# Cross-attention: softmax weights of two heads turned together in row halves, the last head's scores between the V products

## The chip, the cores and the metric

The kernel runs on one core of one Trainium2 chip. The metric is device time in microseconds of one execution; the kernel before takes 1437.06 us (median of three runs, 1436.53 to 1437.17). Five engines work side by side on the core: PE (matrix products; its weight loads are listed apart as PEld), ACT (pointwise functions and casts), DVE (vector arithmetic), POOL (a second, slower vector engine) and SP (which here only starts transfers). Every engine runs its own list of instructions in order and waits on the others by semaphores.

## The reference, cut to what matters

A trunk of two layers on 512 positions of width 1024 in float32. Layer 0 begins with a gated DeltaNet, layer 1 with a convolution module; each layer then has a cross-attention into a fixed memory of 256 rows and a squared-ReLU MLP. The change touches the two cross-attentions alone:

```python
def memory_cross_attention(h, mem_h, w_q, w_kv, w_o):
    B, S, _ = h.shape
    M = mem_h.shape[1]
    q = (h @ w_q).reshape(B, S, XA_HEADS, XA_HEAD_DIM)
    kv = (mem_h @ w_kv).reshape(B, M, 2, XA_HEADS, XA_HEAD_DIM)
    k, v = kv[:, :, 0], kv[:, :, 1]
    s = jnp.einsum("bshd,bmhd->bhsm", q, k).astype(jnp.float32) * (XA_HEAD_DIM ** -0.5)
    p = jax.nn.softmax(s, axis=-1).astype(v.dtype)
    o = jnp.einsum("bhsm,bmhd->bshd", p, v).reshape(B, S, D_MODEL)
    return o @ w_o
```

There are 4 heads of width 256. For one head, the scores are 512 x 256 (positions by memory rows).

## The kernel before, in words

Activations lie with the channels on the 128 partitions and the 512 positions along the row. Each float32 operand of a product is split into a high part (a rounded copy, made by ACT) and a low part (the rest, made by DVE), and each product is done as three: high by high, high by low, low by high. So a 128-row step of a product is three PE rows, and each weight tile of 128 x 1024 needs a cast on ACT (`wh`, L259) and a subtraction on DVE (`wl`, L73).

In a cross-attention, `q_mm(m)` makes 128 of the 1024 query channels (24 PE rows of 512 columns); `q_ev(m)` scales them out of PSUM and splits them. A head takes two such tiles. `sc(h)` makes the scores of head h: four blocks of 128 positions, two to a PSUM bank, 24 PE rows of 256 columns. For each bank DVE takes the negative row maximum (L1128), ACT the exponential and the row sum (L1133, two instructions), DVE the reciprocal (L1136), and POOL multiplies (the `pexp` tile). The scores have the positions on the partitions, but the V product needs the memory rows there, so `tr(h)` turns the weights of a head on PE: eight turns of 128 x 128 against the identity (L1147), four into each of two PSUM banks, one bank for each half of the memory rows; `split` then makes the high part (`pTh`, ACT) and the low part (`pTl`, DVE), each in one instruction of 512 columns. `pv(h)` is the V product, 12 PE rows for each head, whose two outputs are split again (`aoh` on ACT, `aol` on DVE). The output projection `proj(w, outs, ps, k0, k1)` takes those as its steps k: steps 0 and 1 are of head 0, 2 and 3 of head 1, and so on. The first two output tiles (`w0`, `w1`) are begun before all heads are there; six more follow.

The lines at the end of `xattn` write the order of this work out by hand, and PE follows it as written. The order on ACT, DVE and POOL is made by a scheduling layer that takes what is ready in the order of the program and puts it into the engine's list; two engines that read the same PSUM bank are put one behind the other by it. PSUM has 8 banks, shared by all of these tiles (tag `ps`).

Another helper exists before the change: `turn_in` turns a 128 x 128 block in two instructions, one for each half of 64 partitions, each into a PSUM bank of its own (L309). It serves in the DeltaNet, in the convolution module and in the MLP; the tiles turned by it there are `vt`, `ogT`, `lnT` and `hT`. `turned_of` and `by_half` name the pieces in which such a pair of banks is read back.

Of the kernel before, what the change touches and what calls it, by code (L numbers as in the profile page):

```python
# [8 lines left out]
F32 = mybir.dt.float32  # L9
F32R = mybir.dt.float32r  # L10
AF = mybir.ActivationFunctionType
ALU = mybir.AluOpType
AX = mybir.AxisListType

P = 128
# [23 lines left out]
def tile_trunk(ctx, tc, xT, memT, x_d, mem_d, prm_d, adt_d, bdw_d, tap_d, fin_d, first_d, w_ab, w_kq, w_v, w_z, w_dno, w_pw1, w_pw2,  # L39
               w_q, w_k, w_vv, w_o, w_up, w_dn, yT):  # L40
    nc = tc.nc
    pe, act, dve, pool = nc.tensor, nc.scalar, nc.vector, nc.gpsimd
# [11 lines left out]
    def nm(s):  # L54
        cnt[0] += 1
        return f"{s}_{cnt[0]}"

    def slot(dt=F32, s="u", shape=(P, NT)):
        return up.tile(list(shape), dt, tag="u", name=nm(s))

    def psum(s="ps"):
        return psp.tile([P, NT], F32, tag="ps", name=nm(s))

    def small(n, s="sm"):
        return sp.tile([P, n], F32, tag="sm", name=nm(s))

    def const(shape, s, dt=F32):
        return cp.tile(list(shape), dt, tag=s, name=s)
# [3 lines left out]
    def tt(e, o, a, b, op):  # L72
        r = e.tensor_tensor(out=o, in0=a, in1=b, op=op)  # L73
        if e is pool:
            last_pool[:] = [r]
        return r

    def stt(o, a, s, b, op0, op1):
        return dve.scalar_tensor_tensor(out=o, in0=a, scalar=s, in1=b, op0=op0, op1=op1)  # L79
# [6 lines left out]
    def c4(t):  # L86
        return t.rearrange("p (c i) -> p c i", c=4)

    def over_i(t4, n=P):
        return t4.unsqueeze(2).to_broadcast([P, t4.shape[1], n])  # L90
# [34 lines left out]
    ident = const([P, P], "ident")  # L125
# [148 lines left out]
    def wnext(key, hf):  # L274
        i = ws["next"]
        assert order[i] == (key, hf), (order[i], key, hf)
        while ws["load"] <= need[min(i + NRAW + 1 + 2 * (order[i][0][0] in ("up", "dn7")), len(order) - 1)]:
            wload()
        ready = NW - (order[i] == (("do", 1), 1) or i in (conv0 - 1, conv0)) if i > 2 else (1, 2, 1)[i]
        while ws["split"] < min(i + ready, len(order)):  # L280
            wsplit()
        ws["next"] += 1
        return ws["hl"].pop(i)
# [3 lines left out]
    def behind_merge():  # L287
        return tc.issue_after(ahead[0].ins) if ahead else nullcontext()
# [17 lines left out]
    def turn_in(pss, at, src):  # L306
        for half in range(2):
            r = slice(64 * half, 64 * half + 64)
            pe.transpose(pss[half][:, at:at + 64], src[r, :], ident[r, r])  # L309

    def turned_of(pss, k):
        return [c4(ps[:, 256 * k:256 * k + 256]) for ps in pss]

    def by_half(t):
        return [c4(t)[:, :, 64 * half:64 * half + 64] for half in range(2)]

    def mm3(ps, wk, xk, first, last):
        (wh, wl), (xh, xl) = wk, xk
        pe.matmul(ps, wh, xh, start=first, stop=False)  # L319
        pe.matmul(ps, wh, xl, start=False, stop=False)  # L320
        pe.matmul(ps, wl, xh, start=False, stop=last)  # L321

    def wk(w, k):
        c = slice(k * P, (k + 1) * P)
        return w[0][:, c], w[1][:, c]

    def proj(w, xs, ps, k0=0, k1=KT, inside=None):
        for k in range(k0, k1):
            mm3(ps, wk(w, k), xs[k], k == 0, k == KT - 1)
            if inside and k in inside:  # L330
                inside[k]()
# [45 lines left out]
    def split(src, s):  # L377
        h = slot(F32R, s + "h")
        with behind_merge():
            act.copy(h, src)  # L380
        lo = slot(F32R, s + "l")
        tt(dve, lo, src, h.bitcast(F32), ALU.subtract)
        return h, lo
# [708 lines left out]
    def phased(t):  # L1092
        return t.rearrange("p (t s) -> p s t", s=PH)

    def by_phase(t):
        return t.rearrange("p (s t) -> p s t", s=PH)

    def xattn(layer, norm, hres, nxt):
        K, V = KV[layer]
        xs = norm.xs  # L1100
        st = {}

        def q_mm(m, inside=None):
            st["ps", m] = psum("q")
            proj(wnext(("xq", layer, m // 2), m % 2), xs, st["ps", m], inside=inside)

        def q_ev(m):
            qf = slot(s="qf")
            stt(qf, st.pop(("ps", m)), 1.0 / 16, norm.rb, ALU.mult, ALU.mult)
            st["q", m] = split(qf, "q")  # L1110

        def sc(h):
            pr = []
            kh, kl = K[h]
            for tp in range(2):
                ps = psum("sc")
                mxn = small(2)
                for i in range(2):
                    t = tp * 2 + i
                    t_ = slice(t * P, (t + 1) * P)  # L1120
                    o = ps[:, i * 256:(i + 1) * 256]
                    for d in range(2):
                        ks = slice(d * 256, (d + 1) * 256)
                        qh, ql = st["q", 2 * h + d]
                        pe.matmul(o, qh[:, t_], kh[:, ks], start=d == 0, stop=False)
                        pe.matmul(o, qh[:, t_], kl[:, ks], start=False, stop=False)
                        pe.matmul(o, ql[:, t_], kh[:, ks], start=False, stop=d == 1)
                dve.tensor_reduce(out=mxn, in_=ps.rearrange("p (t m) -> p t m", t=2), op=ALU.max,  # L1128
                                  axis=AX.X, negate=True)
                pe_ = slot(s="pexp")  # L1130
                sm = small(2)
                for i in range(2):
                    act.activation(pe_[:, i * 256:(i + 1) * 256], ps[:, i * 256:(i + 1) * 256], AF.Exp,  # L1133
                                   bias=mxn[:, i:i + 1], accum_out=sm[:, i:i + 1])
                rs = small(2)
                dve.reciprocal(rs, sm)  # L1136
                p3 = pe_.rearrange("p (t m) -> p t m", t=2)
                tt(pool, p3, p3, over_i(rs, 256), ALU.mult)
                pr.append(pe_)
            st["p", h] = pr  # L1140

        def tr(h):
            pts = []
            for mt in range(2):
                ps = psum("pT")
                for t in range(4):
                    pe.transpose(ps[:, t * P:(t + 1) * P],  # L1147
                                 st["p", h][t // 2][:, (t % 2) * 256 + mt * P:(t % 2) * 256 + (mt + 1) * P],
                                 ident)
                pts.append(split(ps, "pT"))  # L1150
            st["pt", h] = pts

        outs = [None] * 8

        def pv(h):
            for d in range(2):
                ps = psum("pv")
                for mt in range(2):
                    vh, vl = V[mt, h // 2]
                    vs = slice((h % 2) * 256 + d * P, (h % 2) * 256 + (d + 1) * P)  # L1160
                    mm3(ps, (vh[:, vs], vl[:, vs]), st["pt", h][mt], mt == 0, mt == 1)
                outs[2 * h + d] = split(ps, "ao")

        new = []

        def o_ev(m, ps):
            hn = slot(s="h")
            if layer == 0:
                tt(dve, by_phase(hn), phased(ps), phased(hres[m]), ALU.add)
            else:  # L1170
                tt(dve, hn, ps, hres[m], ALU.add)
            new.append(hn)
            nxt.add(m, hn)

        def ow(m):
            return wnext(("xo", layer, m // 2), m % 2), psum("xo")

        q_mm(0)
        q_mm(1, {1: norm.stat})
        q_ev(0)  # L1180
        q_ev(1)
        q_mm(2); q_ev(2); sc(0)
        q_mm(3); q_ev(3)
        q_mm(4); tr(0); q_ev(4); sc(1)
        q_mm(5); q_ev(5); pv(0)
        q_mm(6); tr(1); q_ev(6); sc(2)
        q_mm(7); q_ev(7); pv(1)
        tr(2)
        w0, p0 = ow(0)
        proj(w0, outs, p0, 0, 4)  # L1190
        sc(3)
        pv(2)
        w1, p1 = ow(1)
        proj(w1, outs, p1, 0, 6)
        tr(3)
        proj(w0, outs, p0, 4, 6)
        pv(3)
        for k in (6, 7):
            proj(w0, outs, p0, k, k + 1)
            proj(w1, outs, p1, k, k + 1)  # L1200
        o_ev(0, p0)
        o_ev(1, p1)
        for m in range(2, 8):
            w, ps = ow(m)
            proj(w, outs, ps)
            o_ev(m, ps)
        return new
# [645 lines left out]
    for gq in range(2):  # L1853
# [9 lines left out]
        for i in range(4):  # L1863
            h = 4 * gq + i
# [55 lines left out]
    h = []  # L1920
# [11 lines left out]
    h = xattn(0, n1, h, n2)  # L1932
    n3 = Norm("cv_norm")
    h, rest = mlp7(0, n2, h, n3, lambda: (mem_gain(1, 0), taps(NTAP, *range(9)), selections()))
    n4 = Norm("xa_norm1")
    h = conformer(n3, h, n4, rest)
    n5 = Norm("mlp_norm1")
    h = xattn(1, n4, h, n5)


# [163 lines left out]
```

## Time and profile before

| | us |
|---|---|
| median of three runs | 1437.06 |
| the profiled execution: its own time | 1436.97 |
| the profiled execution: span from first to last instruction | 1435.3 |
| PE busy | 1426.3 (99%) |
| DVE busy | 1047.7 (73%) |
| ACT busy | 763.0 (53%) |
| POOL busy | 244.2 (17%) |
| cross-attention of layer 0, first q product to the last of the first two output tiles | 346.2 to about 428 |
| the same in layer 1 | about 985 to 1067 |

The granted clock of PE is 0.999 of full speed. In the timeline a PE row of 512 columns is listed with 0.39 us, yet the next one starts 0.23 us later: rows overlap, and what counts is the distance from start to start. The chain of waits (the work that ended last, followed back) lists each step by that distance. "PE xo L320 0.32" there is a row that held up the next by 0.32 us. In names such as `pT<-ident,pexp`, the tile left of the arrow is written and those right of it are read.

### The profile page before, as it was taken

Reading aid. Unit: us, or ns where it says so; the run is one execution under the profiler, and the core shown is the slowest. Engines: PE = TensorE matmul, PEld = TensorE weight load, DVE = VectorE, ACT = ScalarE, POOL = GpSimd, SP = SyncE. Lnnn points to the kernel's source line nnn. Section 1 sums busy time; section 2 is a strip of 40 time slices with the busy share of each in tenths; the row PEclk is TensorE's granted clock in tenths of the full one; section 3 lists DMA queues with packets and bytes.
Section 4 is the critical chain, followed back from the end, with each engine's and each line's share of the span. In section 5 each row is a group of like instructions: output and inputs, shape, how many; then the busy total and the mean of one; then the engine's idle time right before and its main releaser. Section 6 shows DMA issues by size and latency. Waiting matters only on the chain.

```text
span 1435.3 us, 20462 instructions
## 1 busy us (share of the span) xinstructions
PE 1426.3 (99%) x7786; PEld 1191.7 (83%) x7786; DVE 1047.7 (73%) x1625; ACT 763.0 (53%) x1282; POOL 244.2 (17%) x248
## 2 busy tenths in 40 slices
PE   9999999999999999999999999999999999999998
PEld 7887888888888888888888888888888888888886
DVE  5989989867555765767679799976555766767677
ACT  6657855655444454435345656464444644444354
POOL 1212200102113000000000298111112010010101
PEclk9999999999999999999999999999999999999999
DMA  8232235523214567575866448642215476675853
GB/s 292 82 118 66 70 102 162 173 93 103 74 33 129 149 179 179 141 202 134 205 158 219 154 137 291 221 149 89 74 57 134 123 184 166 150 205 138 222 147 88
DMA packets 71860, 207.83 MB, mean 145 GB/s; under 512 B 15441, under 2 KB 16593, under 8 KB 71761
## 3 DMA queue, kind: packets, MB, share of 16 engines
q1 hardware_dynamic: 60960, 169.22, 36.0%
q0 software_dynamic: 9792, 35.66, 14.4%
q10 hardware_dynamic: 1008, 1.64, 0.3%
q8 instruction: 61, 1.00, 0.3%
q14 instruction: 39, 0.31, 0.1%
HBM read 203.28 MB, written 3.21 MB: 144 GB/s over the span
## 4 chain that ended last, share of the span: by engine, by line
PE 90%; DVE 6%; DMA 1%; ACT 1%; issue 1%; POOL 0%; SPq 0%; ACTq 0%; DVEq 0%
PE up L319 8%; PE up L320 8%; PE up L321 8%; PE dn L1263 7%; PE dn L1264 7%; PE dn L1265 7%; PE pw L319 3%; PE pw L320 3%; PE pw L321 3%; PE xo L320 2%; PE q L319 2%; PE xo L319 2%; PE q L320 2%; PE q L321 2%; PE xo L321 2%; PE h L319 1%
## 5 line engine op out<-in xcount | busy, mean ns | idle before, releaser
L259 ACT CAST wh<-raw 128x1024 fp32r<-128x1024 f32 x259 | 271.5, 1051 | 338.0 <-issue 106.6
L73 DVE TENSOR_TENSOR wl<-raw,wh 128x1024 fp32r<-128x1024 f32 (+1 forms) x250 | 306.6, 1229 | 92.7 <-ACT wh L259 91.2
L319 PE MATMUL up<-xh,wh 128*128 128x512 f32 x512 | 199.3, 389 | 0.0
L321 PE MATMUL up<-xh,wl 128*128 128x512 f32 x512 | 199.2, 389 | 0.0
L320 PE MATMUL up<-xl,wh 128*128 128x512 f32 x512 | 199.2, 389 | 0.0
L319 PEld LDWEIGHTS up<-xh,wh 128*128 128x128 f32 x512 | 96.1, 188 | 20.1
L321 PEld LDWEIGHTS up<-xh,wl 128*128 128x128 f32 x512 | 96.1, 188 | 20.0
L320 PEld LDWEIGHTS up<-xl,wh 128*128 128x128 f32 x512 | 96.1, 188 | 19.8
L244 POOL DMA_DIRECT2D t<-w_dn x48 | 42.2, 916 | 375.6 <-DVE wl L73 278.4
L1263 PE MATMUL dn<-wh,ah 128*128 128x512 f32 (+1 forms) x260 | 100.6, 387 | 0.0
L1265 PE MATMUL dn<-wl,ah 128*128 128x512 f32 (+1 forms) x260 | 100.5, 386 | 0.0
L1264 PE MATMUL dn<-wh,al 128*128 128x512 f32 (+1 forms) x260 | 100.4, 386 | 0.0
L79 DVE SCALAR_TENSOR_TENSOR rl<-up,rb 128x512 f32<-128x512 f32 x64 | 44.1, 690 | 58.6 <-PE up L321 58.6
L259 ACT CAST wh<-t 128x1024 fp32r<-128x1024 f32 x44 | 46.5, 1056 | 57.6 <-PE dn L1264 43.7
L73 DVE TENSOR_TENSOR wl<-t,wh 128x1024 fp32r<-128x1024 f32 x44 | 53.7, 1223 | 30.7 <-ACT wh L259 27.2
L73 POOL TENSOR_TENSOR sq<-sq,sq 128x512 f32<-128x512 f32 x26 | 42.8, 1646 | 167.8 <-ACT sq L447 150.6
L73 DVE TENSOR_TENSOR acc<-acc,dn 128x512 f32<-128x512 f32 x99 | 66.6, 681 | 1.0
L319 PE MATMUL h<-xh,wh 128*128 128x512 f32 x160 | 63.8, 399 | 0.0
L1546 DVE SCALAR_TENSOR_TENSOR ca<-xn,prm,ca 128x512 f32<-128x512 f32 x82 | 60.8, 751 | 3.9 <-ACT ca L1543 2.3
L321 PE MATMUL h<-xh,wl 128*128 128x512 f32 x160 | 62.4, 390 | 0.0
L320 PE MATMUL h<-xl,wh 128*128 128x512 f32 x160 | 62.3, 389 | 0.0
L73 DVE TENSOR_TENSOR al<-u,ah 128x512 fp32r<-128x512 f32 x64 | 44.1, 689 | 21.3 <-ACT ah L380 21.3
(425 smaller groups left out, 3493.1 us busy)
## 6 DMA issues: line engine op xcount, KB each, us to landing
raw<-w_dn SPq DMA_DIRECT2D x68, 512.0 KB, 4.6
raw<-w_up SPq DMA_DIRECT2D x64, 512.0 KB, 4.9
t<-w_dn POOLq DMA_DIRECT2D x48, 512.0 KB, 6.4
tap<-tap SPq DMA_DIRECT2D x48, 256.0 KB, 5.7
raw<-w_pw SPq DMA_DIRECT2D x24, 512.0 KB, 4.1
raw<-w_dn POOLq DMA_DIRECT2D x20, 512.0 KB, 7.1
raw<-w_k SPq DMA_DIRECT2D x16, 512.0 KB, 3.9
raw<-w_vv SPq DMA_DIRECT2D x16, 512.0 KB, 5.7
```

What stands on the lines that cost most here:

```text
L73: r = e.tensor_tensor(out=o, in0=a, in1=b, op=op)
L79: return dve.scalar_tensor_tensor(out=o, in0=a, scalar=s, in1=b, op0=op0, op1=op1)
L244: nc.gpsimd.dma_start(out=t, in_=a, accum_op=ALU.add)
L259: ins = [act.copy(h, raw)]
L319: pe.matmul(ps, wh, xh, start=first, stop=False)
L320: pe.matmul(ps, wh, xl, start=False, stop=False)
L321: pe.matmul(ps, wl, xh, start=False, stop=last)
L1263: pe.matmul(ps, xh, w[0][:, s], start=opens and k == 0, stop=False, skip_group_check=True)
L1264: pe.matmul(ps, xl, w[0][:, s], start=False, stop=False, skip_group_check=True)
L1265: pe.matmul(ps, xh, w[1][:, s], start=False, stop=k == 3, skip_group_check=True)
L1546: first["tap"] = dve.scalar_tensor_tensor(out=a, in0=src, scalar=w, in1=a, op0=ALU.mult, op1=ALU.add)
```

## The change

`tr` now takes two heads. It asks for four PSUM banks, turns both heads with `turn_in` (32 turns of 64 partitions by 128 columns, in place of 16 turns of 128 x 128), and then reads the banks back in pieces of 256 columns: for each head and half of the memory rows two copies on ACT and two subtractions on DVE, in place of one and one. In one bank lie both halves of the memory rows for one half of the positions. The order of the steps is another: q tiles 4 to 7 follow each other with only the scores of head 1 between; heads 0 and 1 are turned behind them; then the scores of head 2, V of head 0, the scores of head 3, V of head 1, four steps of the first output tile, the turn of heads 2 and 3, four steps of the second output tile, V of heads 2 and 3, and the steps that are left. What is computed is the same.

```diff
-        def tr(h):
-            pts = []
-            for mt in range(2):
-                ps = psum("pT")
-                for t in range(4):
-                    pe.transpose(ps[:, t * P:(t + 1) * P],
-                                 st["p", h][t // 2][:, (t % 2) * 256 + mt * P:(t % 2) * 256 + (mt + 1) * P],
-                                 ident)
-                pts.append(split(ps, "pT"))
-            st["pt", h] = pts
+        def tr(hs):
+            pss = [[psum("pT") for _ in range(2)] for _ in hs]
+            for h, ps in zip(hs, pss):
+                for mt in range(2):
+                    for t in range(4):
+                        turn_in(ps, (4 * mt + t) * 64,
+                                st["p", h][t // 2][:, (t % 2) * 256 + mt * P:(t % 2) * 256 + (mt + 1) * P])
+            for h, ps in zip(hs, pss):
+                st["pt", h] = []
+                for mt in range(2):
+                    ph, pl = slot(F32R, "pTh"), slot(F32R, "pTl")
+                    for o, lo, x in zip(by_half(ph), by_half(pl), turned_of(ps, mt)):
+                        act.copy(o, x)
+                        tt(dve, lo, x, o.bitcast(F32), ALU.subtract)
+                    st["pt", h].append((ph, pl))
...
-        q_mm(4); tr(0); q_ev(4); sc(1)
-        q_mm(5); q_ev(5); pv(0)
-        q_mm(6); tr(1); q_ev(6); sc(2)
-        q_mm(7); q_ev(7); pv(1)
-        tr(2)
+        q_mm(4); q_ev(4); sc(1)
+        q_mm(5); q_ev(5)
+        q_mm(6); q_ev(6)
+        q_mm(7); q_ev(7)
+        tr((0, 1))
+        sc(2)
+        pv(0)
+        sc(3)
+        pv(1)
         w0, p0 = ow(0)
         proj(w0, outs, p0, 0, 4)
-        sc(3)
+        tr((2, 3))
+        w1, p1 = ow(1)
+        proj(w1, outs, p1, 0, 4)
         pv(2)
-        w1, p1 = ow(1)
-        proj(w1, outs, p1, 0, 6)
-        tr(3)
+        pv(3)
         proj(w0, outs, p0, 4, 6)
-        pv(3)
+        proj(w1, outs, p1, 4, 6)
         for k in (6, 7):
```

**How it moves the rows.** On PE, in layer 0, behind q tile 4, the rows before were these (`pT` the turned weights, `pexp` the weights, `sc` the scores):

```order
L1147 MATMUL pT_4142<-ident,pexp_4045 128x128 x2
L1147 MATMUL pT_4142<-ident,pexp_4067 128x128 x2
L1147 MATMUL pT_4151<-ident,pexp_4045 128x128 x2
L1147 MATMUL pT_4151<-ident,pexp_4067 128x128 x2
L1125 MATMUL sc_4166<-Kh_2732,qh_4026 128x256
```

and now, behind q tile 7, they begin so:

```order
L319 MATMUL q_4266<-xh_3901,wh_4195 128x512
L320 MATMUL q_4266<-xl_3903,wh_4195 128x512
L321 MATMUL q_4266<-xh_3901,wl_4196 128x512
L309 MATMUL pT_4303<-ident,pexp_4045 128x64
L309 MATMUL pT_4304<-ident,pexp_4045 128x64
```

Eight turns of one head behind q tile 4 became 32 turns of two heads behind q tile 7, half as wide, the two partition halves in turn into two banks.

On DVE, in layer 0, behind the eviction of q tile 7, the rows before were these (`aol`: the low part of V of head 1, `pTl`: of the turned weights of head 2, `sm`: maxima and reciprocals of head 3):

```order
L79 SCALAR_TENSOR_TENSOR qf_4399<-q_4368,rb_3961 128x512
L73 TENSOR_TENSOR wl_4448<-raw_4270,wh_4447 128x1024
L73 TENSOR_TENSOR ql_4403<-qf_4399,qh_4401 128x512
L73 TENSOR_TENSOR aol_4414<-pv_4405,aoh_4412 128x512
L73 TENSOR_TENSOR aol_4425<-pv_4416,aoh_4423 128x512
L73 TENSOR_TENSOR pTl_4434<-pT_4427,pTh_4432 128x512
L73 TENSOR_TENSOR pTl_4443<-pT_4436,pTh_4441 128x512
L1128 TENSOR_REDUCE sm_4465<-sc_4464 128x2
L1136 RECIPROCAL sm_4483<-sm_4480 128x2
```

and now they are these (`pTl` of heads 0 and 1, then the maxima of head 2):

```order
L73 TENSOR_TENSOR ql_4301<-qf_4297,qh_4299 128x512
L73 TENSOR_TENSOR pTl_4340<-pT_4303,pTh_4339 128x4x64
L73 TENSOR_TENSOR pTl_4340<-pT_4304,pTh_4339 128x4x64
L73 TENSOR_TENSOR pTl_4346<-pT_4303,pTh_4345 128x4x64
L73 TENSOR_TENSOR pTl_4352<-pT_4305,pTh_4351 128x4x64
L73 TENSOR_TENSOR pTl_4346<-pT_4304,pTh_4345 128x4x64
L73 TENSOR_TENSOR pTl_4352<-pT_4306,pTh_4351 128x4x64
L73 TENSOR_TENSOR pTl_4358<-pT_4305,pTh_4357 128x4x64
L1128 TENSOR_REDUCE sm_4364<-sc_4363 128x2
L73 TENSOR_TENSOR pTl_4358<-pT_4306,pTh_4357 128x4x64
L1136 RECIPROCAL sm_4382<-sm_4379 128x2
L1128 TENSOR_REDUCE sm_4386<-sc_4385 128x2
```

Two wide subtractions of one head became eight half as wide of two heads, and the first maximum of head 2 stands behind seven of them. Behind these rows stand the second reciprocal of head 2, the first maximum of head 3, both `aol` of head 0, the rest of head 3's softmax, and both `aol` of head 1. ACT's list has the same pattern: eight `pTh` copies, the exponentials of head 2, two `aoh`, the exponentials of head 3, two `aoh`. POOL's rows and their order are the same as before, and so are SP's.

## The prediction

> **What bounds the kernel now.** I read the page's busy times and its chain first, then what PE waited for, then PE's time in the stretches that the change touches.
>
> ```profile
> PE 1426.3 (99%) x7786; PEld 1191.7 (83%) x7786; DVE 1047.7 (73%) x1625; ACT 763.0 (53%) x1282; POOL 244.2 (17%) x248
> PE 90%; DVE 6%; DMA 1%; ACT 1%; issue 1%; POOL 0%; SPq 0%; ACTq 0%; DVEq 0%
> PE warm L131 <- POOL ones L128: 1.2, 1, 1.2
> PE mg L780 <- ACT w L790: 0.5, 1, 0.5
> PE rb L421 <- DVE rstd L469: 0.3, 1, 0.3
> 376.80:394.20 17.40, 17.40 (x93) 14.97 (x92) 9.04 (x14) 7.38 (x16) 2.08 (x2) 1.00 0.19 63
> 407.00:424.40 17.40, 17.40 (x94) 15.00 (x93) 6.65 (x12) 5.69 (x15) 2.08 (x2) 1.00 0.08 28
> ```
>
> The first two rows say that PE is the bound: 99% of the span, and 90% of the chain. The next three are the longest of what PE waited for in the whole run (line waited for, total, times, longest); none lies in a cross-attention. The last two are stretches of layer 0's attention: length, then busy PE, PEld, DVE, ACT, POOL, then PE's granted clock. PE is busy for all of 17.40 us at full clock, DVE for 9.04 or 6.65. So what PE is spared there is gained, as long as DVE and ACT still deliver in time; what they do more costs nothing while that holds.
>
> **The turns: removed and added.** The chain of waits gives start, us to the next step, and the step:
>
> ```profile
> 376.76 0.23 PE q L321
> 376.99 0.87 PE pT L1147 x8
> 377.87 0.12 PE sc L1125
> 406.31 0.88 PE pT L1147 x8
> 1058.37 0.87 PE pT L1147 x8
> ```
>
> Eight turns of a head cost 0.87 us, before scores as before 512-wide rows. Four heads in two layers: 8 x 0.87 = 6.97 us go. The new turns have the form of a group that runs already, 32 turns of 64 x 128 between 512-wide rows:
>
> ```profile
> L309 PE MATMUL hT<-ident,h x64: 221/222/272, 1121.0 to 1145.1; 64*128 64x64 f32 x64
> 781.64 1.14 PE hT L309 x32
> 782.78 0.43 PE dn L1263
> 1121.06 1.14 PE hT L309 x32
> 1122.20 0.42 PE up L319
> ```
>
> The group takes 1.14 us, and the row behind it 0.42 or 0.43 where such a row takes 0.23: 0.20 on leaving the form. So 1.34 us for two heads in place of 2 x 0.87 = 1.74, and 4 x 1.34 = 5.36 us in place of 6.97: **1.61 us saved**. Not shown is what leaving the form costs when 256-wide scores follow, as behind heads 0 and 1; the bounds are 0 (the 0.12 row above, behind wide turns) and, as a loss, twice the 0.20. I take 0.20, the nearer case, and keep +-0.4 us in all for both layers.
>
> The Trainium skill, TensorEngine Tiling (Array Packing), Key Properties, says that changing the tiling mode drains the TensorE. The trace agrees as far as the 0.20 us goes; the page has no price, and by its rule the sum stays as it is, since the drain lies in the measured 0.20 and the group is entered only four times.
>
> **Stalls that go.** Just behind `pv(3)` the projection asks for the low part of its output too early, once in each layer:
>
> ```profile
> 424.82 0.32 PE xo L320
> 1063.57 0.32 PE xo L320
> 424.64 0.19 PEld L320 LDWEIGHTS xo<-aol,wh 128*128 128x128 f32 x1 [0.24 <-DVE aol L73]
> ```
>
> 0.32 where the row takes 0.23: 0.09 each. After the change 12 rows (2.7 us) of `proj(w0, 4, 6)` and `proj(w1, 4, 6)` lie between, so **0.18 us** more is saved. The scores, V, q and output rows are the same in number and width, and rows of scores meet rows of 512 as often as before, so I cost their new order at nothing for PE itself.
>
> **What could make PE wait.** ACT and DVE get the turned halves in pieces of 256: for two heads 8 copies and 8 subtractions in place of 4 and 4. These rows (timeline, start and us) price them and the softmax chain:
>
> ```profile
> 403.43 0.39 PE L319 MATMUL pv<-pTh,Vh 128*128 128x512 f32 x1
> 404.40 0.61 ACT L380 CAST qh<-qf 128x512 fp32r<-128x512 f32 x1
> 404.99 0.59 ACT L380 CAST aoh<-pv 128x512 fp32r<-128x512 f32 x1
> 405.67 0.68 DVE L73 TENSOR_TENSOR ql<-qf,qh 128x512 fp32r<-128x512 f32 x1
> 406.27 1.39 DVE L73 TENSOR_TENSOR aol<-pv,aoh 128x512 fp32r<-128x512 f32 x2
> 1122.79 1.18 ACT L1229 COPY acc<-hT 128x256 f32<-128x256 f32 x4
> 783.68 1.41 DVE L73 TENSOR_TENSOR h<-hT,h 128x256 f32<-128x256 f32 x4
> 407.58 1.28 DVE L73 TENSOR_TENSOR pTl<-pT,pTh 128x512 fp32r<-128x512 f32 x2
> 411.39 0.69 DVE L1128 TENSOR_REDUCE sm<-sc 128x2 f32<-128x512 f32 x1 [2.54 <-PE sc L1127]
> 412.18 0.47 ACT L1133 ACTIVATE pexp<-sc,sm 128x256 f32<-128x256 f32 x1 [4.26 <-DVE sm L1128]
> 413.31 0.67 DVE L1128 TENSOR_REDUCE sm<-sc 128x2 f32<-128x512 f32 x1
> 414.02 0.47 ACT L1133 ACTIVATE pexp<-sc,sm 128x256 f32<-128x256 f32 x1 [0.82 <-DVE sm L1128]
> 414.94 1.29 ACT L380 CAST aoh<-pv 128x512 fp32r<-128x512 f32 x2
> 415.07 0.17 DVE L1136 RECIPROCAL sm<-sm 128x2 f32<-128x2 f32 x1 [1.09 <-ACT pexp L1133]
> 415.38 1.04 POOL L73 TENSOR_TENSOR pexp<-pexp,sm 128x512 f32<-128x512 f32 x1 [0.77 <-DVE sm L1136]
> ```
>
> A piece costs 1.18/4 = 0.30 us on ACT, 1.41/4 = 0.35 on DVE. Two heads thus cost DVE 2.8 us in place of 2 x 1.28 = 2.56, ACT 2.4 in place of about 2.2. PE's full stretch covers those 0.24 us; uncovered, four pairs would cost about 1 us.
>
> The length of the serial path matters more. Zero is the end of q tile 7 on PE. In the trace before that is 403.43, the first row below; those at 404 to 406 evict q tile 7 and stay: ACT is free at 1.56, DVE, in whose list the weight split and `ql` come first, at 2.84. Then, layer 0 and 1 alike:
>
> PE: turn 0 to 1.34; scores of head 2, 24 x 0.12, to 4.22; V of head 0, 12 x 0.227, to 6.94; scores of head 3 to 9.82; V of head 1 to 12.54; then the projection. Its eighth row (step 2, low part, from V of head 1) is due at 12.54 + 7 x 0.227 = 14.13, its weight load some 0.2 us ahead: 13.9.
>
> DVE: seven `pTl` of 0.35 put the first maximum of head 2 at 5.3. ACT stays ahead of them, though its third piece must wait for DVE's first, since both read one bank. Then by the rows from 411.39 on: second exponential 2.63 later (7.9), second reciprocal 3.68 later (9.0), first maximum of head 3 at 9.1. Both `aoh` of head 0 (from 8.85 on) and both `aol` (9.7 to 11.0) fit between this maximum and its reciprocal, 1.84 later. Second maximum 1.92 after the first (11.0), its exponential at 11.7, then 0.92 until ACT turns to `aoh` of head 1 (12.6 to 13.2), and `aol` at 13.2 to 13.9.
>
> So it is due at 13.9 and there at 13.9: **just in time**. Some 20 steps may each be off by some hundredths; I put the sum at +-0.4 us, a stall of 0 to 0.5 us in a layer, and take 0.1, **0.2 in all**. The other hand-overs have room. `pv(0)` needs its last `pTl` (the fifth piece, done at 2.84 + 5 x 0.35 = 4.6, or 4.8 with ACT's turns between) at 4.22 + 4 x 0.227 - 0.2 = 4.9. The turn of heads 2 and 3 (due 15.3) needs POOL's last weights, ready at 11.0 + (415.38 + 1.04 - 413.31 = 3.1) = 14.1. `pv(2)` follows that turn by 2.7 us of projection and asks for its fifth piece 0.7 us later, 3.4 us behind the turn; the pieces can begin once head 2 is turned, half a microsecond before the turn ends, and take 5 x 0.35 + 0.3 = 2.1, so 1.8 us are to spare. The weight casts stay one for each 24 rows in the q stretch, and the next two wait for the end of the first two output tiles, as before. What queues behind a late piece is the softmax of heads 2 and 3, and PE waits for that at the projection and the second turn.
>
> **Sum.** -1.61 - 0.18 + 0.2 = -1.6 us. The profiled execution took 1436.97 (span 1435.3); the median shown is 0.09 above it. 1436.97 - 1.6 = 1435.37, or 1435.46 from the median: **1435.4 us**, -0.11%.
>
> **The rivals.** *Evicted late, and slower.* If a piece of 256 costs what a full row does (0.64 on DVE, 1.28/2), the maximum of head 2 comes 7 x 0.29 = 2.0 us later, and PE stands 2.0 us at the projection in each layer; behind the second turn the five pieces, 5 x 0.29 = 1.5 us later, still keep within the room there. Then 2 x 2.0 - 1.8 = +2.2: 1439.2. It decides from 0.9 us of lateness in a layer, where the saving is gone; at 0.5 us the time is 1436.2. For it: the sum above has no slack. Against it: the two rows of 256-wide pieces, one on each engine, both reading such banks. The Trainium skill, TensorEngine Tiling, PSUM Bottleneck, speaks for it: tiling speeds the TensorE but not the emptying of PSUM, and the copy may become the bound. The busy times above, 9.04 of 17.40 us, do not bear that out as a throughput.
>
> *The halves do not overlap.* If each half turn took what a full one takes, 0.87/8 = 0.109, 32 of them would be 3.48 + 0.2, four pairs 14.7 us in place of 6.97: 1444.7. The rows of 1.14 stand against it; only `pexp` as the source is new.
>
> *The saving is swallowed.* PE runs 0.9 us ahead after each attention and waits for it later: 1437.0. Against it: the table of PE's waits, with nothing over 0.5 us behind the start, and no DMA in it.
>
> *More is saved.* To pass 0.2%, 2.9 us, another 1.1 us would have to come from the order; I see no row for it. 1434.0.
>
> **How the numbers follow.** Forecast 75% (1434.6 to 1436.3); late 11%, of which 2% over 1439.9 and the rest between 1436.3 and 1439.2; swallowed 6%; more saved 6%; no overlap 2%. The range, 1434.3 to 1437.1, takes the forecast with its bounds, most of the mild lateness and the swallowed case. About 0.2% (2.9 us) is what a measurement of this kernel can tell from no change. Faster by more: 0.07 (the last but one, and the forecast's far edge); within: 0.89; slower: 0.04 (late, no overlap).
>
> **What would show it.** In the changed kernel's chain: `pT` groups of 32 with 1.14 us, and the row behind them 0.2 too long; no 0.32 row behind `pv(3)`; at the eighth row of the first projection 0.23, or more where `aol` is late, with DVE as PEld's releaser. DVE's seventh `pTl` should start 5 us after q tile 7 and the first maximum at 5.3. Wrong would be: PE idle over 1 us in an attention, a group far from 1.14, or a stage behind the attentions that grew by what these lost.

## The result

The changed kernel takes 1434.43 us (median of 22 runs, 1433.78 to 1436.59); the kernel before takes 1436.53 us (median of 22, 1435.76 to 1438.37). The ratio is 0.9986, with a 95% interval of 0.998 to 0.9992: 2.1 us or 0.14% less, faster beyond the interval, yet inside the 0.2% that the prediction counts as no change. The forecast was 1435.4, range 1434.3 to 1437.1.

The profiled execution's span is 1433.2 us (1435.3 before). The page's busy times and the engines' shares of the chain:

```profile
PE 1424.6 (99%) x7850; PEld 1189.0 (83%) x7850; DVE 1050.0 (73%) x1641; ACT 764.2 (53%) x1298; POOL 244.9 (17%) x248
PE 90%; DVE 6%; DMA 1%; ACT 1%; issue 1%; POOL 0%; SPq 0%; ACTq 0%; DVEq 0%
```

PE is the bound as before. It runs 64 instructions more and is busy 1.7 us less. Where that lies is seen in the two attentions, from the start of the first q product to the start of the MLP's first up product. First the kernel before, then the changed one (stretch, length, then busy PE, PEld, DVE, ACT, POOL, PE's clock, DMA share, GB/s):

```profile
346.24:459.95 113.71, 113.71 (x564) 96.16 (x562) 63.83 (x83) 50.07 (x91) 19.51 (x17) 1.00 0.23 75
984.84:1098.65 113.81, 113.81 (x564) 96.20 (x562) 62.19 (x83) 51.17 (x92) 19.81 (x17) 1.00 0.23 74
```

```profile
346.00:458.75 112.75, 112.75 (x595) 94.88 (x594) 64.41 (x91) 50.73 (x99) 19.52 (x17) 1.00 0.24 75
983.70:1096.57 112.87, 112.87 (x596) 94.93 (x594) 64.01 (x91) 51.69 (x100) 20.45 (x17) 1.00 0.24 75
```

The attentions are 0.96 and 0.94 us shorter, 1.90 in all, at the same clock and with PE busy throughout. What lies between them is as long as before (984.84 - 459.95 = 524.89, now 983.70 - 458.75 = 524.95), and so is the rest behind the second (1435.3 - 1098.65 = 336.65, now 1433.2 - 1096.57 = 336.63). The remaining 0.24 us lies ahead of the first attention (346.24 and 346.00), where nothing was changed; that start lay between 345.2 and 347.8 us in the executions of the experiments below, so 0.24 there is no effect of the change. The same spread of 2.6 us stands in every single time below, which is why the **lengths of the attentions** are compared, and the times only where several rounds were run.

The chain of waits of the changed kernel (start, us to the next step, step), at the two turns of layer 0, at the first rows behind `pv(3)`, and at the turns of layer 1:

```profile
395.97 1.14 PE pT L309 x32
397.11 0.31 PE sc L1125
397.43 0.12 PE sc L1126
...
411.29 1.14 PE pT L309 x32
412.43 0.43 PE xo L319
...
420.83 0.23 PE xo L319
421.06 0.23 PE xo L320
...
1033.78 1.14 PE pT L309 x32
1034.92 0.31 PE sc L1125
...
1049.11 1.14 PE pT L309 x32
1050.25 0.43 PE xo L319
```

All four groups take 1.14. Behind them the first row of scores takes 0.31 where others take 0.12, so the change of form costs 0.19 there; a projection row takes 0.43 in place of 0.23, so 0.20. A group with its exit is 1.33 or 1.34 us. The 0.32 behind `pv(3)` is gone: the first rows after V of heads 2 and 3 run at 0.23.

The chain counts from the end of a row to the end of the next, and so puts the whole 0.19 behind the group. The timeline, which has the starts, divides it:

```profile
395.58 0.39 PE L321 MATMUL q<-xh,wl 128*128 128x512 f32 x1
395.90 1.21 PE L309 MATMUL pT<-ident,pexp 64*128 64x64 f32 x32
397.04 0.38 PE L1125 MATMUL sc<-Kh,qh 128*128 128x256 f32 x1
397.26 0.28 PE L1126 MATMUL sc<-Kl,qh 128*128 128x256 f32 x1
```

The first turn starts 0.32 behind q tile 7's last row, where 0.23 is usual, and the first row of scores holds the next for 0.22, where 0.12 is usual. So about half is paid on entering the form and half on leaving it; the sum is the same.

The just-in-time point is the eighth row of the first projection. The timeline of layer 0, and in the last row the same weight load in layer 1 (start, us, engine, line, operation, and idle time before it with its releaser):

```profile
399.11 1.20 ACT L1154 CAST pTh<-pT 128x256 fp32r<-128x256 f32 x4 [1.17 <-DVE pTl L73]
398.65 2.60 DVE L73 TENSOR_TENSOR pTl<-pT,pTh 128x256 fp32r<-128x256 f32 x7
401.18 0.68 DVE L1128 TENSOR_REDUCE sm<-sc 128x2 f32<-128x512 f32 x1
408.50 1.07 ACT L380 CAST aoh<-pv 128x512 fp32r<-128x512 f32 x2
409.11 1.29 DVE L73 TENSOR_TENSOR aol<-pv,aoh 128x512 fp32r<-128x512 f32 x2 [0.31 <-ACT aoh L380]
409.86 0.19 PEld L320 LDWEIGHTS xo<-aol,wh 128*128 128x128 f32 x1
409.74 0.39 PE L319 MATMUL xo<-aoh,wh 128*128 128x512 f32 x1
409.97 0.39 PE L320 MATMUL xo<-aol,wh 128*128 128x512 f32 x1
...
1047.68 0.19 PEld L320 LDWEIGHTS xo<-aol,wh 128*128 128x128 f32 x1 [0.15 <-DVE aol L73]
```

Q tile 7's last row holds PE until 395.58 + 0.23 = 395.81, the zero of the prediction. The `pTl` start at 398.65 - 395.81 = 2.84, the first maximum at 5.37, `aoh` of head 1 at 12.69. Its two `aol` take 1.29 together; one lasts about 0.68 (a single `ql` of the same size does in this stretch), so the first is done at 409.11 + 0.68 = 409.79, or 13.98. The weight load that needs it starts at 409.86, and its row at 409.97, 0.23 behind the row before, and lasts the usual 0.39. PE did not wait. The weight load did: it starts 0.11 ahead of its row, where the others there start about 0.22 ahead, and in layer 1 it is listed with 0.15 of waiting for `aol`. In the kernel before, the load of the 0.32 row started 0.02 ahead of its row (424.64 and 424.66), and 0.09 was lost. By these two rows hardly anything was left to spare.

### The profile page after: what moved, and what is told of

It is laid out like the page before. It is cut to its first block, busy times and chain, and to the rows that moved or that the text cites. A ratio compares the mean times of both kernels' runs of the same rounds, so it can differ in the third digit from the quotient of the medians.

```text
span 1433.2 us, 20623 instructions
## 1 busy us (share of the span) xinstructions
PE 1424.6 (99%) x7850; PEld 1189.0 (83%) x7850; DVE 1050.0 (73%) x1641; ACT 764.2 (53%) x1298; POOL 244.9 (17%) x248
## 4 chain that ended last, share of the span: by engine, by line
PE 90%; DVE 6%; DMA 1%; ACT 1%; issue 1%; POOL 0%; SPq 0%; ACTq 0%; DVEq 0%
PE up L321 8%; PE up L319 8%; PE up L320 8%; PE dn L1272 7%; PE dn L1274 7%; PE dn L1273 7%; PE pw L319 3%; PE pw L320 3%; PE pw L321 3%; PE xo L319 2%; PE xo L321 2%; PE q L319 2%; PE xo L320 2%; PE q L320 2%; PE q L321 2%; PE h L319 1%
```

## The experiments

The lengths of the two attentions, bounded as above, of every kernel. The last column is from three sets of runs: beside the first four experiments the kernel before took 1436.41 us (19 runs), beside the last three 1436.14 (9).

| kernel | layer 0 | layer 1 | us (runs) |
|---|---|---|---|
| before | 113.71 | 113.81 | 1436.53 (22) |
| the change | 112.75 | 112.87 | 1434.43 (22) |
| order of before, each head in halves | 113.59 | 113.64 | 1436.21 (10) |
| new order, whole turns | 113.53 | 113.65 | 1436.24 (10) |
| all lower halves, then all upper | 114.32 | 114.43 | 1437.47 (1) |
| one maximum taken twice | 113.35 | 113.47 | 1437.85 (1) |
| two maxima taken three times | 114.95 | 115.03 | 1438.74 (8) |
| projection steps ahead of `pv(3)` | 113.07 | 113.10 | 1434.65 (1) |
| scores of head 3 late | 113.77 | 113.80 | 1438.05 (1) |

### The halves alone

The order of before, but each head turned by the new `tr`, 16 half turns to a group. Against the changed kernel:

```diff
-        q_mm(4); q_ev(4); sc(1)
-        q_mm(5); q_ev(5)
...
-        tr((0, 1))
...
+        q_mm(4); tr((0,)); q_ev(4); sc(1)
+        q_mm(5); q_ev(5); pv(0)
+        q_mm(6); tr((1,)); q_ev(6); sc(2)
...
```

> The order of before, but each head turned in row halves (16 turns a head, evicted in pieces of 256). My theory (a group costs 0.036 us a turn and 0.20 on leaving the form): 0.57 + 0.20 = 0.77 in place of 0.87 for each of 8 heads, so an attention of 113.3 us from its first q product to the first up product (before 113.7 and 113.8, after 112.8 and 112.9), 0.8 us less in all than before; the 0.32 row behind pv(3) stays. Rival (the gain is the order's, the halves are worth nothing): 113.7 and 113.8. Rival (the halves are all of it): 112.8.

Measured: 1436.21 us against 1436.41 (median of 19 runs of before beside it), ratio 0.9998 (0.9988 to 1.0007): no difference. The attentions lose 0.12 and 0.17 us, a third of the 0.4 expected. The chain shows why:

```profile
376.12 0.64 PE pT L309 x16
376.76 0.32 PE sc L1125
377.08 0.12 PE sc L1126
```

Sixteen half turns cost 0.64 us, not half of 1.14, and the exit costs the whole 0.20. So a group is 0.84 where a head's eight wide turns took 0.87, and four groups give 4 x 0.03 = 0.12 us, as measured in layer 0; of the 0.05 more in layer 1, 0.04 lies in the scores of head 0, which the edit does not touch. From 16 to 32 turns the group grows by 0.50, so a half turn costs 0.031; then 0.64 - 16 x 0.031 = 0.14 is fixed in the group, and with the exit **0.34 us is paid for each group**, however long. The starts in the trace of the changed kernel tell where: 0.09 ahead of the first turn, 0.05 behind the first two turns, 0.10 behind the last two, 0.10 in the first row behind the group. Halves pay by being many together. The Trainium skill, TensorEngine Tiling (Array Packing), Key Properties, says that a change of the tiling mode drains the TensorE; these rows agree, and a part of the 0.34 may be that drain. Which part isn't settled by them: the trace tells where the time goes, not why.

### The order alone

The new order with the whole turns of before, heads 0 and 1 behind each other, then heads 2 and 3:

```diff
-        tr((0, 1))
+        tr(0)
+        tr(1)
...
-        tr((2, 3))
+        tr(2)
+        tr(3)
```

> The order of after, but heads turned whole, 8 turns of 128 x 128 each, two heads behind each other. My theory: what is left is the stall behind pv(3), 0.09 in a layer, and one entry into the turns fewer for each pair of heads, about 0.09, so an attention of 113.4 to 113.5 us, 0.5 to 0.7 us less in all than before. Rival (the order is what gained): 112.8 to 112.9, 1.9 us less in all.

Measured: 1436.24 us, ratio 1.0 (0.999 to 1.001). The attentions lose 0.18 and 0.16, which is what the two terms of the expectation add up to (0.09 + 0.09), and their lengths, 113.53 and 113.65, lie just above its range. Yet one of the two terms is wrong. In the chain:

```profile
395.65 1.75 PE pT L1147 x16
397.39 0.12 PE sc L1125
```

Sixteen wide turns cost 1.75, twice 0.87: wide turns have nothing fixed, and nothing is gained by joining two heads of them: the 0.09 for an entry fewer is not there, and that the sum came out was luck. What the order gives by itself is the 0.09 of the stall and another 0.07 to 0.09. No single row holds that: from start to start, it is spread over q, score and projection rows, at most 0.01 us in each. The halves alone and the order alone together give 0.30 and 0.33 us in a layer, the change 0.96 and 0.94. So the gain is of neither part: the order lets **two heads share a group**, and only then do halves pay.

### Neighbours on the same half

The 32 half turns of a group in another sequence: first 16 of the lower 64 partitions, then 16 of the upper, where the change lets them alternate.

```diff
-            for h, ps in zip(hs, pss):
-                for mt in range(2):
-                    for t in range(4):
-                        turn_in(ps, ...)
+            for half in range(2):
+                r = slice(64 * half, 64 * half + 64)
+                for h, ps in zip(hs, pss):
+                    for mt in range(2):
+                        for t in range(4):
+                            at, c = (4 * mt + t) * 64, (t % 2) * 256 + mt * P
+                            pe.transpose(ps[half][:, at:at + 64], st["p", h][t // 2][r, c:c + P], ident[r, r])
```

> After, but in each group the 16 turns of the lower 64 partitions come first and then the 16 of the upper, so that neighbours use the same half. My theory (two neighbours on different halves overlap): a turn then costs at least the 0.071 us that a pair costs now, a group 2.3 us or more in place of 1.14, each attention 2.3 us longer, 115.1. Rival (a turn of 64 columns costs 0.036 us by its width alone): group 1.14, attention 112.8.

Measured in one run; the attentions are 114.32 and 114.43 us, 1.57 and 1.56 above the change and longer than before. The chain:

```profile
395.40 1.93 PE pT L1150 x32
397.33 0.32 PE sc L1125
```

1.93 in place of 1.14; 2 x 0.79 = 1.58 is the whole of the difference. With the fixed 0.14 off, a half turn costs (1.93 - 0.14) / 32 = 0.056 us on average, against 0.031 where halves alternate. The starts in the trace say more. Here the turns follow each other by 0.062 us, but for the ends of the group and the changeover from one half to the other, where three turns start within 0.007 us of a neighbour. In the change the turns run in pairs: the second starts 0.003 to 0.009 us behind the first, and the next pair 0.062 behind this one. So a pair costs no more than a single half turn does here. The neighbours do overlap, almost wholly, and it is this overlap that earns the gain: two half turns that don't overlap, 2 x 0.062 = 0.124, cost more than one wide one, 0.87 / 8 = 0.109. My price for a half turn without overlap was at least 0.071; hence the miss in size. Neighbours on one half also write into one PSUM bank here, and those that alternate into two. The run does not separate the half from the bank.

### One maximum more on the just-in-time path

The second maximum of head 2 is taken twice, which changes nothing in what is computed:

```diff
-                dve.tensor_reduce(out=mxn, ...)
+                for _ in range(1 + ((h, tp) == (2, 1))):
+                    dve.tensor_reduce(out=mxn, ...)
```

> After, with the second row maximum of head 2 taken twice on DVE, 0.6 us more on the path from q tile 7 to aol of head 1; PE's own work is unchanged. My theory (aol comes just in time for the eighth row of the first projection): PE stands 0.5 to 0.6 us there, an attention of 113.3 to 113.5 us. Rival (there is slack of 0.6 us or more): 112.8 and 112.9.

Measured in one run: 113.35 and 113.47, 0.60 above the change, within what was expected. It is not the plain stall that I had in mind. The timeline of PE at the first projection, the weight load of its seventh row first:

```profile
411.67 0.19 PEld L319 LDWEIGHTS xo<-aoh,wh 128*128 128x128 f32 x1 [0.41 <-ACT aoh L380]
411.30 0.39 PE L321 MATMUL xo<-aoh,wl 128*128 128x512 f32 x1
411.67 0.49 PE L319 MATMUL xo<-aoh,wh 128*128 128x512 f32 x1
412.10 0.46 PE L309 MATMUL pT<-ident,pexp 64*128 64x64 f32 x8
412.49 0.50 PE L320 MATMUL xo<-aol,wh 128*128 128x512 f32 x1
...
413.84 0.97 PE L309 MATMUL pT<-ident,pexp 64*128 64x64 f32 x24
```

The seventh row starts 0.37 behind the sixth, 0.14 too late: its weight load waited for `aoh` of head 1. It then lasts 0.49 in place of 0.39, another 0.10. And eight turns of head 2 now stand between the seventh and the eighth: the group is cut in two. So PE's list is not always the written order. The scheduling layer brought turns forward; why just these, the trace does not tell (my guess is that it held them to be ready sooner than `aol`). The eight turns take 412.49 - 412.10 = 0.39 us, what 0.14 + 8 x 0.031 gives, so the price of a group holds for this length too. The cut costs the fixed 0.34 once more, and 0.14 + 0.10 + 0.34 = 0.58 of the 0.60. This confirms that there is no slack for 0.7 us, but more than half of the lateness shows itself as a cut group and not as waiting.

### Nearly three microseconds more

Both maxima of head 2 taken three times: four more of 0.7 us.

```diff
-                for _ in range(1 + ((h, tp) == (2, 1))):
+                for _ in range(1 + 2 * (h == 2)):
```

> After, with both row maxima of head 2 taken three times on DVE: about 2.9 us more on the path from q tile 7 to aol of head 1 (0.72 us for each, by the run with one), in each attention. The scheduling layer has also put turns of head 2 ahead of rows of the first projection in PE's list. My theory (no slack on that path): PE stands about 2.9 us less what the moved turns fill, some 1 us, so an attention of 114.5 to 115.7 us against 112.8, and the whole slower than before by 1 to 4 us. Rival (a late path is filled by other work): below 113.4.

Measured: 1438.74 us (8 runs) against 1436.14, ratio 1.0019 (1.0008 to 1.0031): slower than before, as expected. The attentions are 2.2 us longer than the change's, and 1.2 longer than before. What weight loads waited for in layer 0 (line waited for, us in total, times, longest):

```profile
PEld pT L309 <- issue: 1.3, 4, 0.4
PEld pT L309 <- POOL pexp L73: 0.7, 2, 0.5
PEld xo L319 <- ACT aoh L380: 0.4, 1, 0.4
```

The first row is no lateness: it stands ahead of groups of turns in the change as well, with 0.7 in all. The second turn is cut into four groups (three groups more, about 1.0 of the 2.2 at 0.34 each), and what PE waits for besides is the softmax of heads 2 and 3 and the output split of head 1: the two places that the prediction named for a late piece. "Evicted late" is a real way to lose this change; it did not happen here because the pieces were as cheap as forecast.

### The rows between `pv(3)` and its use

Of the 12 projection rows behind `pv(3)`, those of steps 4 and 5 go ahead of it again:

```diff
         pv(2)
+        for k in (4, 5):
+            proj(w0, outs, p0, k, k + 1)
+            proj(w1, outs, p1, k, k + 1)
         pv(3)
-        proj(w0, outs, p0, 4, 6)
-        proj(w1, outs, p1, 4, 6)
```

> After, but with steps 4 and 5 of the first two output tiles between V of head 2 and V of head 3, so that each V product is followed at once by the steps that read it. My theory: the 0.32 row behind pv(3) comes back, and there is one behind pv(2) as well, 0.09 us each, an attention of 112.9 to 113.0 us. Rival (those rows had another cause, or ACT and DVE are emptier now): 112.8.

Measured in one run: 113.07 and 113.10, 0.32 and 0.23 above the change and a little more than expected. The chain has the stalls back:

```profile
417.54 0.31 PE xo L320
423.14 0.32 PE xo L320
```

One is behind `pv(3)`, as in the kernel before, the other where step 4 now follows `pv(2)` at once. They make 0.08 + 0.09 = 0.17; the other 0.06 to 0.15 is in no single row: it is spread over projection rows, at most 0.02 us in each. The cause of the stall, a low part asked for too soon, holds.

### Where the last head's scores stand

The scores of head 3 moved out from between the V products to behind the first four projection steps, the second turn moved behind the second four:

```diff
         pv(0)
-        sc(3)
         pv(1)
         w0, p0 = ow(0)
         proj(w0, outs, p0, 0, 4)
-        tr((2, 3))
+        sc(3)
         w1, p1 = ow(1)
         proj(w1, outs, p1, 0, 4)
+        tr((2, 3))
```

> After, but with the scores of head 3 behind V of heads 0 and 1 and the first projection, and the second output tile's four steps between them and the turn of heads 2 and 3. From the end of a head's scores to POOL's last weights the trace of before takes 3.8 us; here 2.8 us of projection and 0.6 us of head 2's turns lie between. My theory (the place of these scores is what keeps the softmax off PE's path): PE stands about 0.4 to 0.6 us in the turn, an attention of 113.2 to 113.5 us. Rival (their place does not matter): 112.8.

Measured in one run: 113.77 and 113.80, as long as before; more than expected. What weight loads waited for in layer 0:

```profile
PEld xo L320 <- DVE aol L73: 0.5, 1, 0.5
PEld pT L309 <- POOL pexp L73: 0.3, 1, 0.3
PEld pv L319 <- ACT pTh L1154: 0.3, 1, 0.3
```

Three stalls where the change has none. The first is at the second row of the projection, which reads the low part of V of head 0: the 2.9 us of scores that stood between V of head 0 and the projection are gone, and both V products' splits come in one go (the first `aol` starts at 406.61, the load that needs it at 407.35). The softmax of head 3 comes too close before its turn, and V of head 2 too close behind it. The blocks of PE rows at these places are 0.4, 0.4 and 0.25 us longer than in the change, together the 1.0 us of the difference. So the gain stands and falls with the written order: with the same turns in the same groups, one misplaced block of scores gives all of it back.

## Why the prediction held, and where it was off

- **PE is the bound**: right. The whole saving is PE time in the attentions, and nothing swallows it later: the stretch between the attentions and that behind them are unchanged within 0.06 us.
- **A group at 1.34 with its exit**: right as a sum, though half of what it puts on leaving the form is paid on entering it. 1.14 + 0.20 before projection rows, and 1.14 + 0.19 before scores, the unknown that was taken at 0.20 within bounds of 0 and 0.40. Four pairs give 4 x (2 x 0.87) - 2 x (1.33 + 1.34) = 1.62 us; forecast 1.61. It was right because a group of the same length was at hand. Scaled from it by the turn, as I did for the halves alone, it missed: 0.77 against 0.84.
- **The stall behind `pv(3)`**: right, 0.09 in each layer, and it comes back when the rows between are taken away.
- **Just in time**: right to a tenth of a microsecond. The first maximum at 5.37 (forecast 5.3), `aoh` of head 1 at 12.69 (12.6), the first `aol` done at 13.98 (13.9).
- **The stall of 0.2 us taken for it**: this term was mis-sized; it is 0. The row ran at its usual 0.23, although `aol` came at 13.98, later than the 13.9 at which the prediction had it due. It had put the weight load some 0.2 ahead of its row; a load 0.11 ahead was enough.
- **The new order costs PE nothing**: mis-sized by little. By the sum, 1.62 + 0.18 = 1.80 of the 1.90 us is accounted for, and the order gives the other 0.10, 0.05 in a layer; the order alone gave 0.07 to 0.09, spread over many rows.
- **The absolute time**: 1434.43 is 0.97 below the forecast. Of that, 0.53 is the base (the median of 22 runs of before is 1436.53, that of the three shown 1437.06), 0.20 the stall that wasn't, 0.10 the order; the other 0.14 is less than what the part ahead of layer 0 varies by.
- **The rivals**: "evicted late" did not occur, since the seven pieces took (401.18 - 398.65) / 7 = 0.36 us each, and not 0.64. The Trainium skill, TensorEngine Tiling (Array Packing), PSUM Bottleneck, warns that after a speedup by tiling (it names 4x) the copy out of PSUM may become the bottleneck. The trace bears that out only as a latency, at one point of the path, as the two kernels with more maxima show. "Do not overlap" is excluded by 1.14 against 1.93 in the same place, and its price would have been 0.062 for a half turn, and not 0.109. "Swallowed" is excluded by the unchanged stretches. "More is saved" is right in direction only: 2.1 us and not 2.9.

Open are why rows run some hundredths of a microsecond faster in the new order (0.05 to 0.09 us in a layer), what makes the 0.34 fixed in a group, and whether neighbours overlap for their different halves or for their different banks.

## What to carry to other kernels

Price a group of half-row turns as a whole, with its exit: about 0.34 + 0.031 us for each half turn here, against 0.109 for a wide turn, so that eight wide turns replaced by 16 halves gain next to nothing (0.03) and 16 replaced by 32 gain 0.4 us. Let neighbours alternate between the halves, and gather enough of them in one place before doing it at all. When the order is rewritten to gather them, follow the slowest serial path (turn, copy, split, softmax, split) step by step from durations in the trace; here that told the arrival of the last piece to 0.1 us, and lateness of one maximum costs most of the gain.

## What the hardware showed that I had not expected

- A group of half-row turns has a fixed cost of 0.34 us (0.14 inside, 0.20 at its two ends), where wide turns have none (8 in 0.87, 16 in 1.75).
- A half turn behind one on the same half costs 0.062 us, more than half of a wide turn's 0.109, and a pair on different halves costs the same 0.062: the second of the pair is free. The prediction had taken a half turn without overlap for as dear as a wide one.
